# A third couple of groups in the up projections, later restores of the residual, parking at first chunks

## The chip, the cores and the metric

One core of a Trainium2 chip runs the whole program. The metric is device microseconds from the first to the last instruction of one launch, as the median of several runs; less is better.

## The reference

The program computes two layers of a streaming encoder on 256 positions of width 2048, batch 1, all in float32. Each layer is a token mixer and a gated feed-forward part, each followed by a residual and a layer norm:

```python
for i in range(DEPTH):                       # DEPTH = 2
    m = gmlp_mixer(x, ...) if i % 2 == 0 else mla_mixer(x, ...)
    x = layer_norm(ALPHA * x + m, ln_mix_g[i], ln_mix_b[i])
    f = conv_ffn(x, ffn_w_up[i], ffn_conv_w[i], ffn_conv_b[i], ffn_w_down[i])
    x = layer_norm(ALPHA * x + f, ln_ffn_g[i], ln_ffn_b[i])
```

The change concerns the feed-forward part, `conv_ffn`: `h = x @ w_up` (2048 x 11008), a causal depthwise convolution of width 3 over the positions of `h`, then `(silu(g) * a) @ w_down` with `a` and `g` the two halves of `h` (5504 each).

## The kernel before

**Products.** TensorE multiplies in a reduced float32 form, so each weight chunk `raw` (1 MB, read on SyncE's DMA queue, SP) is split in two parts: ScalarE casts it to `wh` (line 134) and VectorE subtracts, `wl = raw - wh` (line 137). The activations `xhl` are kept as such pairs too. `Feed.next` hands out the next chunk and lets the loads run up to four chunks and the splits two chunks ahead.

**Up projection.** Its columns come in 22 groups (0 to 21) of 4 chunks each (the last is half a group). Group 0 is done beside the layer norm ahead of it (`boundary`). The others are *plain* or in *couples*, as the table `UP` says. A plain group (`plain`) multiplies each chunk 16 times with 512 columns for `wh` and 256 for `wl`, accumulates four tiles `up{layer}_{group}_{f}`, and ends with two `pair`s: sum of halves `h_`, convolution `c_`, `silu`, and product into `act`. A couple (`summed`) takes 8 chunks of two groups. Four of them go as in `eight`, 24 matmuls of 512 columns. The other four (`UP_SEVEN`) use a scheme of seven products in place of eight, 21 matmuls of 512 columns; for them VectorE also makes sums of weight blocks, `ts` (line 144), and splits those into `th` and `tl`, and it needs combined inputs `xu`, made beforehand by `combine_up` (one `upy`, four `xsu`, one cast and one `xu`). After a couple come `rest` and four adds on VectorE, then, behind the first chunk of the next plain group, 16 transposes (`turn_back`, tiles `upr`), and the couple's four `pair`s behind its second and third chunk (`both`).

**Side work, by a table.** `EARLY` maps (group, chunk) to steps done beside the plain groups: `restore f` scales and shifts a quarter `f` of the residual that the layer norm left unscaled (its gain and bias rows `lnp` are DMA loads, then two multiplies and two adds of 128x512), `combine i` is above, and `park h` writes a half of the residual to DRAM on GpSimd's queue (`resd`), after which its room (tiles `res` and `sum`) is free. The other side work is `jobs`: eight chunks of the later down projection ("parked", `praw`, numbers 231 to 266) are loaded, split as for seven products (`pwh`, `pwl`, `pth`, `ptl`), and written to DRAM (`keptwh`, ...), one step at a time, 31 steps in all.

**Order.** Each engine works in the order of its own instruction stream, which follows from the order of these calls and from the scheduler of the framework. Rooms come from pools by tag: "big" has 14 of 2048 columns, "side" 6, "raw" 3. `behind(load)` asks that a load be queued after the latest matmul so far; it adds no wait.

Layer 0's up projection has chunks 144 to 229. Chunks 148 to 151 are group 1, and 152 to 155 group 2.

Of the kernel before, what the change touches and what calls it, by code (L numbers as in the profile page):

```python
# [15 lines left out]
P = 128  # L16
# [53 lines left out]
LEAD = 5  # L70
KEEP = {"wide": 4, "seven": 6, "parked": 6}

UP = [(1,), (2,), (3,), (4,), (5, 6), (7,), (8, 9), *((i,) for i in range(10, 22))]
UP_PAIRS = [0, 2, 1, 3, 5, 4, 6, 7]
UP_SEVEN = (2, 3, 4, 6)
EARLY = {(1, 2): ("restore", 0), (2, 1): ("combine", 0), (2, 2): ("restore", 1), (2, 3): ("park", 0),
         (3, 1): ("restore", 2), (3, 2): ("combine", 1), (3, 3): ("restore", 3), (4, 0): ("park", 1),
         (4, 1): ("combine", 2), (4, 2): ("combine", 3)}


def plan(n_k):
# [140 lines left out]
def trunk(ctx: ExitStack, tc: tile.TileContext, x, xT, gm_in, gm_wout, ffn_up, ffn_dn,  # L222
# [12 lines left out]
    def slot(shape, name, dt=F32, tag="big"):  # L235
        return big.tile(shape, dt, tag=tag, name=name, bufs=SLOTS[tag])
# [13 lines left out]
    def behind(ins):  # L250

        if recent[0] is not None and feed.used > 0:
            order(ins, recent[0])
# [424 lines left out]
    class Norm:  # L678
# [53 lines left out]
        def restore(self, f):  # L732

            row = []
            for j in range(2):
                t = tp.tile([P, 512], F32, tag="t2", name=f"lnp{self.idx}_{f}{j}", bufs=T2)
                src = ln_rows[2 * self.idx + j : 2 * self.idx + j + 1, f * 512 : (f + 1) * 512]
                (nc.gpsimd if self.idx == 1 else nc.sync).dma_start(t, src.to_broadcast([P, 512]))
                row.append(t)
            for b in range(2):  # L740
                nc.vector.tensor_tensor(self.r(b, f), self.r(b, f), row[0], ALU.mult)
                nc.vector.tensor_tensor(self.r(b, f), self.r(b, f), row[1], ALU.add)
# [287 lines left out]
    def ffn(layer, ln, acc, end, last):  # L1030
# [39 lines left out]
        def combine_up(p):  # L1070

            x = xhl[p // 2][:, p % 2 * 2 : p % 2 * 2 + 2]
            y = tp.tile([P, 2, S], F32, tag="t2", name=f"upy{layer}_{p}", bufs=T2)
            nc.vector.tensor_tensor(y, x[:, :, 0:S].bitcast(F32), x[:, :, S : 2 * S].bitcast(F32), ALU.add)
            if len(sums) % 2 == 0:
                rooms.append(slot([P, 2, 8 * P], f"xu{layer}_{p}", F32R))
            sums[p] = combine(f"u{layer}_{p}", rooms[-1][:, len(sums) % 2, :], y[:, 0], y[:, 1])

        early = {"restore": old.restore, "park": old.park, "combine": lambda i: combine_up(UP_SEVEN[i])}
# [1 line left out]
        def plain(gi, turned):  # L1081

            nt, nk = (4, 4) if gi < 21 else (2, 8)
            acc = [bank(f"up{layer}_{gi}_{f}") for f in range(nt)]
            for c in range(KD // nk):
                hi, lo = feed.next()
                prod_a(acc, xhl, range(nk * c, nk * c + nk), hi, lo)
                if c == 0 and turned:
                    for i, t in enumerate(turned[2]):
                        turn_back(turned[1][i % 2], t, i // 2)  # L1090
                if turned and 0 < c < 3:
                    both(turned[0][c - 1], turned[1][c - 1])
                if (gi > 9 and c > 0) or (gi, c) == (7, 3):
                    next(jobs, None)
                if (gi, c) in FIRST:
                    acts.make(*plan(NF_FF)[0][FIRST.index((gi, c))])
                if gi == 1 and c == 0:
                    after(1, 1, None)
                    both(0, hb)
                if (gi, c) in EARLY:  # L1100
                    name, i = EARLY[gi, c]
                    early[name](i)
            for f in range(nt // 2):
                pair(2 * gi + f, acc[f], acc[nt // 2 + f])
# [456 lines left out]
```

## Time and profile before

| what | value |
|---|---|
| median of 3 runs | 2450.4 us (2450.39 to 2450.6) |
| profiled execution, its own time | 2449.38 us |
| its span, first to last instruction | 2447.3 us |
| granted TensorE clock | 1.00 |
| busy: TensorE / VectorE / ScalarE / GpSimd | 100% / 90% / 62% / 6% |
| DMA over the span, mean | 256 GB/s |

Times in views of the profile count from the start of the span. Layer 0's up projection lies between about 780 and 1264 us, layer 1's from about 1735 on. PE is TensorE, DVE VectorE, ACT ScalarE, POOL GpSimd, SP SyncE. A duration of an instruction includes its way through the engine, so two that follow each other overlap a little. L137 is line 137 of the kernel before; in the changed kernel all lines from 739 on stand two lower down.

### The profile page before, as it was taken

The page shows a single profiled execution, that of the slowest core. Times are in us where ns is not written, and L with a number is a line of the kernel's source. Part 1 is how long each engine was busy: PE and PEld are TensorE (multiplying, and loading weights), DVE is VectorE, ACT ScalarE, POOL GpSimd, SP SyncE. Part 2 cuts the span into 40 slices and gives each one's busy share as a digit, 9 for nine tenths or more (in the row PEclk, how much of TensorE's full clock was granted, in tenths as well). Part 3 has the DMA queues.
Part 4 walks back from the last instruction along what each step waited for, and adds up shares of the span by engine and source line. Part 5 has one row for each costly group of instructions (what it writes and reads, how often), then busy time and mean ns, then how long its engine had stood idle before and what let it go on. Part 6 is the DMA issues. An engine that isn't in the chain of part 4 may idle for free.

```text
span 2447.3 us, 32249 instructions
## 1 busy us (share of the span) xinstructions
PE 2440.4 (100%) x12151; PEld 2065.3 (84%) x12151; DVE 2191.0 (90%) x2914; ACT 1512.4 (62%) x1997; POOL 140.6 (6%) x261
## 2 busy tenths in 40 slices
PE   9999999999999999999999999999999999999999
PEld 7888888888888888888888888988888888888887
DVE  7999999899998889998889897878798999888998
ACT  6666665566576655666665566665655666666553
POOL 0000000001010000011000000000000001010000
PEclk9999999999999999999999999999999999999999
DMA  7555666658796755799988885533575589898894
GB/s 293 203 205 205 233 202 205 207 173 304 254 296 241 239 205 194 258 359 374 341 318 320 320 298 172 188 141 126 207 272 184 181 323 375 321 371 300 314 353 178
DMA packets 128763, 627.37 MB, mean 256 GB/s; under 512 B 11592, under 2 KB 15184, under 8 KB 91616
## 3 DMA queue, kind: packets, MB, share of 16 engines
q1 hardware_dynamic: 94224, 462.47, 53.5%
q0 software_dynamic: 34384, 162.86, 17.9%
q8 instruction: 95, 1.56, 0.3%
q14 instruction: 60, 0.49, 0.1%
HBM read 552.35 MB, written 72.93 MB: 256 GB/s over the span
## 4 chain that ended last, share of the span: by engine, by line
PE 97%; DVE 1%; DMA 1%; ACT 0%; issue 0%; POOL 0%; ACTq 0%; DVEq 0%; POOLq 0%
PE up L242 30%; PE ub L242 16%; PE dn_q L242 8%; PE dn_p L242 6%; PE v_q L242 5%; PE v_p L242 4%; PE up_q L242 3%; PE up_p L242 3%; PE wo_q L242 2%; PE dn_e L242 2%; PE wo_p L242 2%; PE upf L242 2%; PE mo L242 2%; PE v_e L242 2%; PE mkv L242 1%; PE qn L242 1%
## 5 line engine op out<-in xcount | busy, mean ns | idle before, releaser
L137 DVE TENSOR_TENSOR wl<-raw,wh 128x1024 fp32r<-128x1024 f32 (+5 forms) x611 | 936.3, 1550 | 108.9 <-ACT wh L134 77.4
L134 ACT CAST wh<-raw 128x1024 fp32r<-128x1024 f32 (+5 forms) x611 | 790.9, 1318 | 307.2 <-PE up L242 67.8
L242 PE MATMUL up<-xhl,wh 128*128 128x512 f32 x2112 | 492.9, 390 | 0.0
L242 PEld LDWEIGHTS up<-xhl,wh 128*128 128x128 f32 x2112 | 392.3, 188 | 78.7
L134 ACT CAST th<-ts 128x1536 fp32r<-128x1536 f32 x196 | 203.7, 1051 | 173.9 <-DVE ts L144 144.2
L242 PEld LDWEIGHTS up<-xhl,wl 128*128 128x128 f32 x2112 | 262.4, 192 | 5.1
L242 PE MATMUL up<-xhl,wl 128*128 128x256 f32 x2112 | 265.1, 283 | 0.0
L137 DVE TENSOR_TENSOR tl<-ts,th 128x1536 fp32r<-128x1536 f32 x196 | 231.6, 1219 | 7.9 <-ACT th L134 3.3
L242 PE MATMUL ub<-wh,xhl 128*128 128x512 f32 x552 | 172.0, 393 | 0.0
L144 DVE TENSOR_TENSOR ts<-ts,raw 128x512 f32<-128x512 f32 x196 | 134.7, 687 | 2.0
L242 PEld LDWEIGHTS ub<-wh,xhl 128*128 128x128 f32 x552 | 103.6, 188 | 23.2 <-issue 1.9
L144 DVE TENSOR_TENSOR ts<-raw 128x1024 f32<-128x1024 f32 x98 | 119.5, 1219 | 2.2 <-DMA raw<-in_gm_in_dram 0.8
L242 PE MATMUL ub<-wl,xhl 128*128 128x512 f32 x276 | 107.5, 389 | 0.0
L242 PE MATMUL v_q<-wh,xhl 128*128 128x512 f32 x224 | 70.8, 391 | 0.0
L242 PEld LDWEIGHTS ub<-wl,xhl 128*128 128x128 f32 x276 | 51.8, 188 | 10.9
L242 PE MATMUL v_p<-wh,xhl 128*128 128x512 f32 x192 | 59.9, 389 | 0.0
L242 PEld LDWEIGHTS v_q<-wh,xhl 128*128 128x128 f32 x224 | 42.1, 188 | 9.7 <-ACT wh L134 0.9
L832 ACT ACTIVATE lny<-lnt,lncol 128x128 f32<-128x128 f32 x96 | 36.6, 471 | 15.7 <-PE lnt L828 15.6
L161 DVE TENSOR_TENSOR praw<-praw 128x512 f32<-128x512 f32 x64 | 43.9, 686 | 0.5
L242 PE MATMUL v_q<-wl,xhl 128*128 128x512 f32 x112 | 43.6, 389 | 0.0
L242 PE MATMUL mo<-wh,oT 128*128 128x512 f32 x128 | 42.7, 411 | 0.0
L242 PEld LDWEIGHTS v_p<-wh,xhl 128*128 128x128 f32 x192 | 36.0, 188 | 7.5
(2073 smaller groups left out, 4824.9 us busy)
## 6 DMA issues: line engine op xcount, KB each, us to landing
raw<-in_ffn_up_dram SPq DMA_DIRECT2D x172, 1024.0 KB, 5.9
raw<-in_gm_in_dram SPq DMA_DIRECT2D x93, 1024.0 KB, 5.3
raw<-in_ffn_dn_dram SPq DMA_DIRECT2D x68, 1024.0 KB, 7.7
raw<-in_gm_wout_dram SPq DMA_DIRECT2D x48, 1024.0 KB, 6.4
praw<-in_ffn_dn_dram POOLq DMA_DIRECT2D x16, 1024.0 KB, 12.5
keptth<-pth POOLq DMA_DIRECT2D x16, 1024.0 KB, 8.5
kepttl<-ptl POOLq DMA_DIRECT2D x16, 1024.0 KB, 8.7
fth<-keptth POOLq DMA_DIRECT2D x16, 1024.0 KB, 9.5
```

What stands on the lines that cost most here:

```text
L134: cast = self.nc.scalar.copy(hi, raw)
L137: self.nc.vector.tensor_tensor(lo, raw, hi.bitcast(F32), ALU.subtract)
L144: add = lambda o, a, b: self.nc.vector.tensor_tensor(o, a, b, ALU.add)
L161: add = lambda o, a, b: pin(nc.vector.tensor_tensor(o, a, b, ALU.add))
L242: recent[0] = nc.tensor.matmul(o, l, r, start=start, stop=stop, skip_group_check=True)
L832: nc.scalar.activation(y[:, j], t[:, j * P : (j + 1) * P], AF.Identity, bias=lncol[:, o : o + 1], scale=lncol[:, g : g + 1])
```

## The change

```diff
-UP = [(1,), (2,), (3,), (4,), (5, 6), (7,), (8, 9), *((i,) for i in range(10, 22))]
+UP = [(1,), (2,), (3, 4), (5,), (6, 7), (8,), (9, 10), *((i,) for i in range(11, 22))]
 UP_PAIRS = [0, 2, 1, 3, 5, 4, 6, 7]
 UP_SEVEN = (2, 3, 4, 6)
-EARLY = {(1, 2): ("restore", 0), (2, 1): ("combine", 0), (2, 2): ("restore", 1), (2, 3): ("park", 0),
-         (3, 1): ("restore", 2), (3, 2): ("combine", 1), (3, 3): ("restore", 3), (4, 0): ("park", 1),
-         (4, 1): ("combine", 2), (4, 2): ("combine", 3)}
+EARLY = {(1, 1): ("restore", 0), (1, 2): ("combine", 0), (1, 3): ("combine", 1), (2, 0): ("restore", 1),
+         (2, 1): ("combine", 2), (2, 2): ("park", 0), (2, 3): ("combine", 3),
+         (12, 0): ("restore", 2), (14, 0): ("restore", 3), (14, 2): ("park", 1)}
@@ Norm.restore
-                (nc.gpsimd if self.idx == 1 else nc.sync).dma_start(t, src.to_broadcast([P, 512]))
+                load = (nc.gpsimd if self.idx == 1 else nc.sync).dma_start(t, src.to_broadcast([P, 512]))
+                if f > 1 and self.idx != 1:
+                    behind(load)
@@ ffn, combine_up
-                rooms.append(slot([P, 2, 8 * P], f"xu{layer}_{p}", F32R))
+                rooms.append(slot([P, 2, 8 * P], f"xu{layer}_{p}", F32R, "side"))
@@ ffn, plain
-                if (gi > 9 and c > 0) or (gi, c) == (7, 3):
+                if (gi > 10 and (c > 0 or 15 < gi < 19)) or (gi, c) == (8, 3):
                     next(jobs, None)
```

In both layers the couples become (3,4), (6,7) and (9,10) where they were (5,6) and (8,9). The four combines, restores 0 and 1 and the first park move into groups 1 and 2; restores 2 and 3 and the second park move to groups 12 and 14. Parking starts with one step in group 8 and goes on from group 11 (before: 7 and 10), and in groups 16 to 18 it also has a step at the first chunk; it ends at the same place. The rooms of `xu` come from "side" instead of "big".

The first place is VectorE after the convolutions of group 1. Before, chunks 157 to 159 are plain ones of groups 3 and 4 and stand among the restores of the residual:

```order
L742 TENSOR_TENSOR res0_0_4680<-res0_0_4680,lnp0_11_6545 128x512
L137 TENSOR_TENSOR wl157_6552<-raw157_6459,wh157_6551 128x1024 x2
L741 TENSOR_TENSOR sum0_1_5777<-sum0_1_5777,lnp0_20_6715 128x512 x2
L742 TENSOR_TENSOR sum0_1_5777<-sum0_1_5777,lnp0_21_6717 128x512
L137 TENSOR_TENSOR wl158_6636<-raw158_6509,wh158_6635 128x1024 x2
L742 TENSOR_TENSOR sum0_1_5777<-sum0_1_5777,lnp0_21_6717 128x512
L1074 TENSOR_TENSOR upy0_3_6763<-xhl1_1_5899 128x512
L137 TENSOR_TENSOR wl159_6676<-raw159_6557,wh159_6675 128x1024
```

With the change, behind the same convolutions (an upy and its xsu are a combine, ts and tl belong to a seven-product chunk):

```order
L1076 TENSOR_TENSOR upy0_4_6520<-xhl1_2_5900 128x512
L137 TENSOR_TENSOR wl156_6531<-raw156_6438,wh156_6530 128x2048
L314 TENSOR_TENSOR xsu0_4_6523<-upy0_4_6520 128x128
L315 TENSOR_TENSOR xsu0_4_6523<-upy0_4_6520 128x128
L144 TENSOR_TENSOR ts157_6570<-raw157_6486 128x1024
L316 TENSOR_TENSOR xsu0_4_6523<-xsu0_4_6523,upy0_4_6520 128x128
L144 TENSOR_TENSOR ts157_6570<-ts157_6570,raw157_6486 128x512
L317 TENSOR_TENSOR xsu0_4_6523<-upy0_4_6520,xsu0_4_6523 128x128
L137 TENSOR_TENSOR wl157_6572<-raw157_6486,wh157_6571 128x1536
L326 TENSOR_TENSOR xu0_4_6522<-xsu0_4_6523,xu0_4_6522 128x512
L137 TENSOR_TENSOR tl157_6574<-ts157_6570,th157_6573 128x1536
L137 TENSOR_TENSOR tl157_6574<-ts157_6570,th157_6573 128x512
```

The last two combines now stand between the splits of the first couple, the second half of the residual is not touched here any more, and chunk 157 has become a seven-product chunk.

The second place is group 12. On SyncE's queue the rows of restore 2 stand behind the load of chunk 196:

```order
L109 DMA raw195_8273<-in_ffn_up_dram 128x2048
L109 DMA raw196_8363<-in_ffn_up_dram 128x2048
L738 DMA lnp0_20_8397<-in_ln_rows_dram 128x512
L738 DMA lnp0_21_8399<-in_ln_rows_dram 128x512
L109 DMA raw197_8411<-in_ffn_up_dram 128x2048
```

Before, they stood there behind the load of chunk 157, ahead of that of 158. On VectorE the restore itself now stands between the parking of chunk 231 (praw, ptl), the convolutions of group 11 and the split of chunk 195:

```order
L161 TENSOR_TENSOR praw231_7740<-praw231_7740 128x512
L1028 SCALAR_TENSOR_TENSOR c_0a22_8319<-h_0a22_8317,cst_176,c_0a22_8319 128x254
L411 TENSOR_TENSOR h_0g22_8325<-up0_11_2_8071,lo_0g22_8323 128x256
L743 TENSOR_TENSOR sum0_1_5777<-sum0_1_5777,lnp0_20_8397 128x512 x2
L744 TENSOR_TENSOR sum0_1_5777<-sum0_1_5777,lnp0_21_8399 128x512
L173 TENSOR_TENSOR ptl231_8308<-praw231_7740,pth231_8307 128x2048
L1026 SCALAR_TENSOR_TENSOR c_0g22_8327<-h_0g22_8325,cst_176,c_0g22_8327 128x255
L744 TENSOR_TENSOR sum0_1_5777<-sum0_1_5777,lnp0_21_8399 128x512
L1028 SCALAR_TENSOR_TENSOR c_0g22_8327<-h_0g22_8325,cst_176,c_0g22_8327 128x254
L137 TENSOR_TENSOR wl195_8406<-raw195_8273,wh195_8405 128x1024
```

Here a multiply and an add of the residual came into a place that had none.

## Prediction, made before the changed kernel ran

> **What bounds the kernel now.** I read the page first: busy shares, then the chain of waits.
>
> ```profile
> span 2447.3 us, 32249 instructions
> PE 2440.4 (100%) x12151; PEld 2065.3 (84%) x12151; DVE 2191.0 (90%) x2914; ACT 1512.4 (62%) x1997; POOL 140.6 (6%) x261
> PE 97%; DVE 1%; DMA 1%; ACT 0%; issue 0%; POOL 0%; ACTq 0%; DVEq 0%; POOLq 0%
> ```
>
> TensorE (PE) is busy almost throughout and is 97% of the chain. So matmuls taken away come back as time, but VectorE (DVE), which prepares every operand and stands at 90%, has little to lend. Which of the two decides is seen in the stage, so next I read the chain through layer 0's up projection (start, duration, what) and the same rows of layer 1.
>
> ```profile
> 816.36 83.36 PE up L242 x480
> 899.72 1.36 PE up_q L242 x6
> ...
> 939.16 1.36 PE up_q L242 x6
> 940.52 5.54 PE up L242 x32
> 946.06 1.75 PE upr L1049 x16
> 947.81 16.68 PE up L242 x96
> 964.49 1.36 PE up_q L242 x6
> ...
> 1005.64 5.54 PE up L242 x32
> ```
> ```profile
> 1771.00 83.36 PE up L242 x480
> 1900.70 1.75 PE upr L1049 x16
> ```
>
> The chain never leaves PE here: 480 plain matmuls without a gap, then couple (5,6) from 899.72 to 940.52, 16 transposes, a plain group, couple (8,9) from 964.49 to 1005.64. Layer 1 repeats the 83.36 and the 1.75, so I cost one layer and double it. Third, the busy time by stretch: groups 2, 3, 4, couple (5,6), groups 11 and 12, and groups 11 to 20 together (columns: PE, PEld, DVE, ACT, POOL busy, granted clock, DMA share, GB/s).
>
> ```profile
> 833.60:855.80 22.20, 22.20 (x130) 19.66 (x129) 21.15 (x36) 12.48 (x20) 0.55 (x1) 1.00 0.89 296
> 855.80:878.00 22.20, 22.20 (x129) 19.67 (x128) 20.80 (x41) 12.58 (x20) 1.26 (x2) 1.00 0.70 240
> 878.00:899.70 21.70, 21.70 (x127) 19.26 (x126) 17.63 (x26) 10.67 (x17) 0.00 (x0) 1.00 0.67 223
> 899.70:940.50 40.80, 40.80 (x182) 33.78 (x181) 37.04 (x43) 25.36 (x27) 0.00 (x0) 1.00 0.53 185
> 1029.60:1051.80 22.20, 22.20 (x130) 19.66 (x129) 20.29 (x29) 13.17 (x17) 2.87 (x5) 1.00 0.98 362
> 1051.80:1074.10 22.30, 22.30 (x130) 19.75 (x129) 20.67 (x29) 13.75 (x20) 2.88 (x5) 1.00 1.01 420
> 1118.50:1140.80 22.30, 22.30 (x130) 19.73 (x129) 19.30 (x28) 13.37 (x20) 1.78 (x3) 1.00 0.99 383
> 1029.60:1251.90 222.30, 222.30 (x1282) 196.90 (x1281) 195.86 (x274) 142.09 (x196) 22.61 (x40) 1.00 0.94 357
> ```
>
> PE fills every stretch at clock 1.00. DVE's cover is 1 to 4 us per group, and DMA is nearly full from group 11 on. These two are what the change draws on.
>
> **What goes: matmuls.** A group is 4 chunks of 32 matmuls, so by the 480-matmul row it takes 83.36 x 128/480 = 22.23 us, two of them 44.46. A couple takes 940.52 - 899.72 = 40.80 and its transposes 1.75. One more couple per layer gains 44.46 - 42.55 = 1.91 us, both layers **3.82 us**. That is the most the change can give: nothing else on PE becomes less. The Trainium skill's "TensorE: Matmul & The Clock Gate", section "Back-to-back issue gap", gives an isolated matmul of N columns N/2.4 + 2.5 ns, which would make the gain about 1.0 us an estimate per layer (128 pairs of 512 and 256 columns against 180 of 512). The 1.36 us for six are 227 ns each, not 216, so the measured rows decide.
>
> **What moves forward: DVE before the first couple.** Couple (3,4) starts 44.46 us earlier than (5,6) did, at 899.72 - 44.46 = 855.26, and four combines must be done by then. The orders of DVE agree up to the subtraction at 822.94. I count from there to the last difference (`tl`) of chunk 162, the fourth seven-product chunk. Three wide chunks of 24 x 0.227 = 5.44 and three seven-product ones of 21 x 0.227 = 4.76 precede it on PE, and PE wants that second part some 2.5 us into the chunk: 855.26 + 30.6 + 2.5 = 888.4, which leaves 65.5 us.
>
> ```profile
> 808.58 3.49 DVE L137 TENSOR_TENSOR wl<-raw,wh 128x1024 fp32r<-128x1024 f32 x3
> 822.94 1.22 DVE L137 TENSOR_TENSOR wl<-raw,wh 128x1024 fp32r<-128x1024 f32 x1
> 824.41 1.29 DVE L741 TENSOR_TENSOR res<-res,lnp 128x512 f32<-128x512 f32 x2
> 832.80 0.42 DVE L411 TENSOR_TENSOR h_0a<-up,lo_0a 128x256 f32<-128x256 f32 x1 [0.76 <-ACT lo_0a L409]
> 839.58 0.48 DVE L1024 SCALAR_TENSOR_TENSOR c_0a<-h_0a,cst,c_0a 128x255 f32<-128x255 f32 x1 [0.47 <-ACT c_0a L1023]
> 846.54 0.42 DVE L1041 TENSOR_TENSOR act<-s,c_0a 128x256 f32<-128x256 f32 x1 [0.28 <-ACT s L1040]
> 847.82 2.36 DVE L137 TENSOR_TENSOR wl<-raw,wh 128x1024 fp32r<-128x1024 f32 x2 [0.25 <-PE up L242]
> 872.01 2.36 DVE L137 TENSOR_TENSOR wl<-raw,wh 128x1024 fp32r<-128x1024 f32 x2 [0.17 <-issue]
> 875.70 0.28 DVE L317 TENSOR_TENSOR xsu<-upy,xsu 128x128 f32<-128x128 f32 x1
> 875.90 0.28 DVE L315 TENSOR_TENSOR xsu<-upy 128x128 f32<-128x128 f32 x1
> 880.69 1.23 DVE L137 TENSOR_TENSOR wl<-raw,wh 128x1024 fp32r<-128x1024 f32 x1 [3.85 <-DMA resd<-sum]
> 886.59 2.29 DVE L137 TENSOR_TENSOR wl<-raw,wh 128x2048 fp32r<-128x2048 f32 x1
> 894.50 0.43 DVE L1041 TENSOR_TENSOR act<-s,c_0a 128x256 f32<-128x256 f32 x1
> 894.85 1.75 DVE L137 TENSOR_TENSOR wl<-raw,wh 128x1536 fp32r<-128x1536 f32 x1
> 896.52 2.35 DVE L137 TENSOR_TENSOR tl<-ts,th 128x1536 fp32r<-128x1536 f32 x2
> ```
>
> Instructions overlap, so I count start to start: 1.135 us per 1024 columns (three in 3.49, the last 1.22), 0.60 per 512 (1.29 for two), 1.67 per 1536 (894.85 to 896.52), 2.2 per 2048 (886.59 to the next at 888.80), 0.20 per 128, 0.35 per `act`, and for the convolutions' two-step pairs 0.39, their durations of 0.48 less the same overlap. Before chunk 162's end the new order has 7 half splits (7.9 us), 3 whole ones (6.6), four seven-product chunks (1.14 + 2 x 0.60 + 1.67 + 1.67 + 0.60 = 6.28 each, 25.1), four combines (2 x 0.60 + 4 x 0.20, some 2.2 with their small gaps; 8.8), 8 restore operations (4.8), and 8 `h`, 16 convolution and 5 `act` operations (10.7). Together 64.0 of the 65.5 us. If DVE idles as long as now without the wait for the residual's store (0.76 + 0.47 + 0.28 + 0.25 + 0.17 = 1.93 us), PE stalls 64.0 + 1.93 - 65.5 = 0.4. If it idles with the 3.85 too, 4.3. With no idling, nothing. I take **0.4**, since the store of the other half, now issued earlier in group 2, held up no DVE instruction in any of these rows; the bounds are 0 and 4.3.
>
> **Third couple.** Couple (8,9) took 1005.64 - 964.49 = 41.15, 0.35 over (5,6): only one plain group lies ahead of it, and the four convolutions and adds of the couple before fall there. Couples (6,7) and (9,10) now both lie so. One more such stall: **0.35**, bounds 0 and 0.70.
>
> **Late residual rows, groups 11 to 13.** Restore 2 goes to group 12's first chunk, where a couple's pairs and the first parking steps already stand on DVE. Its four operations take 2.4 us, and group 11 of before had 22.20 - 20.29 = 1.9 us free. If nothing else gave, the stall would be 0.5; DVE runs up to two chunks ahead, so some is absorbed. The rows that it needs are now loaded behind chunk 196.
>
> ```profile
> DMA to landing us min/median/max: 4.9/6.2/7.3
> raw<-in_ffn_up_dram SPq DMA_DIRECT2D x37, 1024.0 KB, 8.8
> keptth<-pth POOLq DMA_DIRECT2D x8, 1024.0 KB, 8.6
> praw<-in_ffn_dn_dram POOLq DMA_DIRECT2D x6, 1024.0 KB, 12.8
> ```
>
> The first row is the loads of these rows in groups 1 to 3, the others are issues from group 11 to the end of the stage. The load can go out once chunk 193's split has freed a room, and on DVE 9.9 us of work then lie ahead of the restore (`act` and four convolution steps 1.9, chunk 194 2.3, half of 195 1.1, and the rest up to it). At 6.2 to 8.8 us plus issue the rows come just in time; at 12.8 DVE waits 2.9 us, with the splits of 195 to 198 queued behind it and PE behind those. I take **0.4** for both, bounds 0 and 2.9. Restore 3 and the second park, at group 14, have one couple's pairs fewer beside them. The park's store frees the room for chunk 205's split: 8.6 us by the `keptth` row against the 11 us that two chunks last, as the 3.85 us at 880.69 cost PE nothing, so 0.
>
> **Denser parking, groups 16 to 18.** Thirty-one steps, starting one group later and ending at the same place, put four into each of three groups. With a step in every chunk and four steps per parked chunk, a group asks for 4 raw loads, one `praw` and stores of 2 x 1024 and 2 x 768 KB: 8704 KB, 8.91 MB in 22.23 us or 401 GB/s, against the mean of 357. Group 12 moved 420 in 22.30 us. I take **0.1**; bounds 0 and 3.0, the latter if three such groups get only the 383 GB/s of the 1118.50 row, whose DMA share was already 0.99: 26.74 MB/383 = 69.8 us against 66.7. The fourth step is a quarter of a parked chunk's DVE work (1.67 + 4 x 0.60 + 2.2 = 6.3), 1.6 us, and the 1118.50 row leaves 3.0 free.
>
> **Rest, at nothing.** The rooms of the combined inputs change from one pool to another that is empty of parked chunks until group 8; were it short, only the first `praw` would be late. The first half's rows land as before.
>
> **Sum.** Per layer -1.91 + 0.4 + 0.35 + 0.4 + 0.1 = -0.66 us, both -1.3. The profiled execution took 2449.38 us, its span 2447.3 plus 2.1 around it; by it 2448.1. The median of the runs is 2450.4 (2450.39 to 2450.6), 1.0 above it, so the forecast is 2450.4 - 1.3 = **2449.1 us**.
>
> **Rivals.** *Full gain*: DVE's run-ahead swallows all four terms, 2450.4 - 3.8 = 2446.6. For it: PE is at 22.20 of 22.20 in the stretches with DVE at 21.15. Against it: couple (8,9) did lose 0.35. 20%.
>
> *DMA full in groups 16 to 18*: the 3.0 instead of 0.1, per layer +2.2, 2454.9. For it: shares of 0.99 to 1.01 at 383 and 420 GB/s. Against it: the 420. 7%. With the long mean of 357 as the true limit, the three groups last 26.74/0.357 = 74.9 us, 8.2 over, and the time is 2450.4 + 2 x 7.4 = 2465; group 12 speaks against it, 1%. The Trainium skill's "DMA: Bandwidth & Descriptors", section "Where 436 GB/s comes from", states such a limit, about 358 GB/s for transfers between HBM and SBUF; the 420 in group 12 disagrees with it as a limit of this core.
>
> *Slower, the first couple waits for DVE*: the 4.3 of above instead of 0.4, per layer +3.2, both +6.5, 2456.9. Its place is chunk 162, its mechanism the store of the first residual half that now frees a room for chunk 157's casts just as the couple's operands are made; ScalarE waits for it with the third combine's cast queued behind. From 2.6 us of idle time on DVE between 822.94 and 888.4 the kernel is slower than before (a stall of 1.1 uses up what the other terms leave of the 1.91), from 5.0 us by over 0.2%. For it: the 3.85 wait of the same kind. Against it: a store of that size took 8.6 us in busier groups, and by the same spacings some 11 us of DVE work lie between the restore and the first operand that needs chunk 157's cast. 10%.
>
> **How the numbers follow.** Forecast 62%, full gain 20%, DMA 8%, slower 10%. The forecast's own range, its four terms between 0 and twice their size, is 2446.6 to 2451.6. The range to hold 8 in 10 goes from 2446.4 to 2453.2: the full gain with 0.2 for the runs' spread, and above it partial sizes of the two slow cases; their far ends, about 15%, are left out. A measurement of this kernel tells about 0.2%, 4.9 us, from no change, so 2445.5 to 2455.3 is the same. The full gain lies within it: faster 3%. Slower needs the last rival or the 357 limit, 8%. Same 89%.
>
> **What would show it.** After: PE rows of couples at 855, 920 and 985 us; `up` matmuls before the first falling from 480 to about 224; the first couple 40.8 to 41.2 long, with a stall at chunk 162 if any; groups 12 and 13 over 22.23; groups 16 to 18 near 400 GB/s with PE still full. A couple over 42 us, or a `wl` or `th` waiting for the residual's store by more than 3 us, would make the prediction wrong; so would a gain over 3.8.

## The result, and the profile after

The changed kernel takes **2467.74 us** (median of 6 runs, 2465.74 to 2469.43) beside 2450.5 for the kernel before: **ratio 1.0070, interval 1.0058 to 1.0083**. It is 17 us slower, where 2449.1 was forecast in a range of 2446.4 to 2453.2. The profiled execution took 2465.74 us with a span of 2463.7. First its page:

```profile
span 2463.7 us, 32050 instructions
PE 2442.6 (99%) x12031; PEld 2061.3 (84%) x12031; DVE 2221.7 (90%) x2938; ACT 1518.3 (62%) x1983; POOL 140.2 (6%) x261
PE 80%; DVE 10%; DMA 5%; ACT 2%; issue 2%; SPq 0%; ACTq 0%; DVEq 0%
```

PE was 97% of the chain and is 80%: VectorE, DMA and ScalarE have come into it. The 120 matmuls are gone (12151 to 12031), yet PE's busy time has grown by 2 us, a first sign that some matmuls run slower. Where, the chain through layer 0's up projection shows (start, duration, what):

```profile
816.73 38.90 PE up L242 x224
855.63 1.36 PE up_q L242 x6
...
896.58 5.54 PE up L242 x32
902.12 1.75 PE upr L1051 x16
...
920.54 1.36 PE up_q L242 x6
...
961.67 5.54 PE up L242 x32
...
985.63 1.36 PE up_q L242 x6
...
1026.43 5.54 PE up L242 x32
...
1042.99 1.11 issue
1044.10 1.75 DVE pwl L173
1048.60 7.94 DMA raw<-in_ffn_up_dram
...
1271.89 1.36 PE dn_q L242 x6
```

The three couples are nearly perfect: 40.95, 41.13 and 40.80 us, and at their end (1026.43) the layer is 209.70 us past its 816.73. Before, the end of group 10 came 83.36 + 40.80 + 23.97 + 41.15 + 23.97 = 213.25 us past its 816.36 (a group with transposes is 5.54 + 1.75 + 16.68 = 23.97). That is 3.55 more; the third couple's transposes, 1.75, are still to come, so **1.80 us are gained by then**. From there on the chain leaves PE, and the first down product comes at 1271.89, 455.16 us past 816.73; before, 1012.93 + 250.06 - 816.36 = 446.63. So 8.53 us are lost in sum, **10.3 us of them behind the third couple**. In layer 1:

```profile
1779.74 38.91 PE up L242 x224
...
1989.43 5.54 PE up L242 x32
...
2234.06 1.36 PE dn_q L242 x6
```

The same: 1989.43 - 1779.74 = 209.69, then 2234.06 - 1779.74 = 454.32 against 2217.67 - 1771.00 = 446.67 before, so 7.65 lost in sum, 9.5 behind the couples. The two layers together, 16.2, are nearly all of the span's growth of 16.4. Next PE itself, in order of time (start, duration, matmuls, and in brackets the idle time ahead and its releaser):

```profile
1109.43 3.03 PE L242 MATMUL up<-xhl,wl 128*128 128x256 f32 x24
1115.71 1.21 PE L242 MATMUL up<-xhl,wl 128*128 128x256 f32 x8 [3.24 <-DVE wl L137]
1116.76 9.04 PE L242 MATMUL up<-xhl,wh 128*128 128x512 f32 x32
...
1217.98 1.22 PE L242 MATMUL up<-xhl,wl 128*128 128x256 f32 x8 [0.39 <-DVE wl L137]
...
1252.98 1.80 PE L242 MATMUL up<-xhl,wl 128*128 128x256 f32 x8 [2.35 <-DVE wl L137]
1255.23 1.88 PE L242 MATMUL up<-xhl,wl 128*128 128x256 f32 x8 [0.45 <-DVE wl L137]
```

PE waits for VectorE mainly in two places: at the last chunk of group 14 and, near the end of the stage, at the last chunk of group 20 (with a short wait in group 19). The waits are 3.24 + 0.39 + 2.35 + 0.45 = 6.4 of the 10.3 us. Of the other 3.9, some 2.8 are slow matmuls: behind the first wait 32 of them take 9.04 us, elsewhere 7.44, and the two groups of eight at the end take 1.80 and 1.88, elsewhere 1.22 beside a wait. The rest is the broken stream itself, about 0.26 at each of the four waits: 32 such matmuls take 3.84 us from start to start without a break (1042.75 to 1046.59), eight of them 0.96. What VectorE did ahead of that first wait:

```profile
1105.41 0.47 DVE L1028 SCALAR_TENSOR_TENSOR c_0g<-h_0g,cst,c_0g 128x254 f32<-128x254 f32 x1
1108.96 1.29 DVE L743 TENSOR_TENSOR sum<-sum,lnp 128x512 f32<-128x512 f32 x2 [3.08 <-DMA lnp<-in_ln_rows_dram]
...
1112.11 1.29 DVE L744 TENSOR_TENSOR sum<-sum,lnp 128x512 f32<-128x512 f32 x2 [1.18 <-DMA lnp<-in_ln_rows_dram]
...
1114.44 1.22 DVE L137 TENSOR_TENSOR wl<-raw,wh 128x1024 fp32r<-128x1024 f32 x1
```

It stands still for the rows of restore 3 (two multiplies and two adds, as restore 2 has in group 12), and the split that PE needs (`wl` at 1114.44) is queued behind. For the rows of restore 2 it had waited only 0.42 us. The four loads of layer 0 took longer than in groups 1 to 3 (minimum, median, maximum):

```profile
DMA to landing us min/median/max: 8.9/10.1/13.0
```

### The profile page after: what moved, and what is told of

It is laid out like the page before. It is cut to its first block, busy times and chain, and to the rows that moved or that the text cites. A ratio compares the mean times of both kernels' runs of the same rounds, so it can differ in the third digit from the quotient of the medians.

```text
span 2463.7 us, 32050 instructions
## 1 busy us (share of the span) xinstructions
PE 2442.6 (99%) x12031; PEld 2061.3 (84%) x12031; DVE 2221.7 (90%) x2938; ACT 1518.3 (62%) x1983; POOL 140.2 (6%) x261
## 4 chain that ended last, share of the span: by engine, by line
PE 80%; DVE 10%; DMA 5%; ACT 2%; issue 2%; SPq 0%; ACTq 0%; DVEq 0%
PE ub L242 16%; PE up L242 10%; PE dn_q L242 8%; PE dn_p L242 6%; PE v_q L242 5%; PE up_q L242 5%; DVE wl L137 4%; PE up_p L242 4%; PE v_p L242 4%; DMA raw<-in_ffn_up_dram 3%; PE wo_q L242 2%; PE dn_e L242 2%; PE wo_p L242 2%; PE upf L242 2%; PE mo L242 2%
## 5 line engine op out<-in xcount | busy, mean ns | idle before, releaser
L137 DVE TENSOR_TENSOR wl<-raw,wh 128x1024 fp32r<-128x1024 f32 (+4 forms) x595 | 929.7, 1578 | 96.0 <-ACT wh L134 79.7
L134 ACT CAST wh<-raw 128x1024 fp32r<-128x1024 f32 (+4 forms) x595 | 785.8, 1342 | 279.3 <-DMA raw<-in_ffn_up_dram 81.8
L242 PE MATMUL up<-xhl,wh 128*128 128x512 f32 x1856 | 436.6, 392 | 1.0 <-ACT wh L134 1.0
L242 PEld LDWEIGHTS up<-xhl,wh 128*128 128x128 f32 x1856 | 346.6, 189 | 71.2 <-ACT wh L134 1.4
L134 ACT CAST th<-ts 128x1536 fp32r<-128x1536 f32 x212 | 220.7, 1052 | 201.5 <-DVE ts L144 176.7
L137 DVE TENSOR_TENSOR tl<-ts,th 128x1536 fp32r<-128x1536 f32 x212 | 250.5, 1217 | 4.2 <-PE v_p L242 1.9
L242 PE MATMUL up<-xhl,wl 128*128 128x256 f32 x1856 | 237.4, 285 | 12.3 <-DVE wl L137 12.3
L242 PEld LDWEIGHTS up<-xhl,wl 128*128 128x128 f32 x1856 | 232.9, 193 | 18.4 <-DVE wl L137 13.8
L242 PE MATMUL up_q<-wh,xhl 128*128 128x512 f32 x192 | 59.5, 389 | 0.0
L242 PE MATMUL up_p<-wh,xhl 128*128 128x512 f32 x192 | 59.1, 389 | 0.0
L242 PEld LDWEIGHTS v_q<-wh,xhl 128*128 128x128 f32 x224 | 42.0, 188 | 10.3 <-ACT wh L134 1.7
```

What stands on the lines that cost most here:

```text
L134: cast = self.nc.scalar.copy(hi, raw)
L137: self.nc.vector.tensor_tensor(lo, raw, hi.bitcast(F32), ALU.subtract)
L242: recent[0] = nc.tensor.matmul(o, l, r, start=start, stop=stop, skip_group_check=True)
```

## The experiments

Every kernel was timed beside the kernel before on the same chip. The column "against before" is the difference of the medians.

| kernel | median us | against before | ratio, 95% interval |
|---|---|---|---|
| changed kernel | 2467.74 | +17.2 | 1.0070 (1.0058 to 1.0083) |
| late restores only, on before | 2456.37 | +6.5 | 1.0026 (1.0016 to 1.0036) |
| parking only, on before | 2454.35 | +4.5 | 1.0018 (1.0009 to 1.0028) |
| changed, no first-chunk steps | 2471.15 | +21.3 | 1.0091 (1.0076 to 1.0106) |
| changed, rows not behind products | 2454.79 | +5.0 | 1.0021 (1.0011 to 1.0030) |
| changed, no late restores | 2448.11 | -2.5 | 0.9988 (0.9979 to 0.9997) |
| changed, restores in groups 5 and 8 | 2451.75 | +1.2 | 1.0006 (0.9997 to 1.0016) |
| changed, no parked sums | 2452.37 | +1.8 | 1.0007 (0.9997 to 1.0017) |
| changed, half the stores | 2450.80 | +0.2 | 1.0002 (0.9992 to 1.0011) |
| restores on GpSimd, groups 5 and 8 | 2456.70 | +6.6 | 1.0029 (1.0019 to 1.0038) |
| restores on GpSimd, groups 12 and 14 | 2464.55 | +14.4 | 1.0053 (1.0038 to 1.0069) |
| restores at last chunks of 5 and 8 | 2451.77 | +1.6 | 1.0006 (0.9997 to 1.0015) |
| changed, rows' loads earlier | 2466.79 | +16.6 | 1.0064 (1.0050 to 1.0078) |
| restores in 5, 5 and 8 by halves | 2450.88 | +0.7 | 1.0002 (0.9993 to 1.0011) |
| restores at second chunks of 5 and 8 | 2452.05 | +1.9 | 1.0005 (0.9997 to 1.0014) |
| restores at first chunks of 5 and 8 | 2451.73 | +1.6 | 1.0004 (0.9996 to 1.0013) |
| restore work without rows | 2456.05 | +5.9 | 1.0024 (1.0014 to 1.0033) |
| rows and waits without work | 2455.34 | +5.2 | 1.0024 (1.0014 to 1.0033) |

**Which part of the change.** Two kernels put one part on the kernel before, two take one part from the changed kernel.

Late restores only, on the kernel before (with the `behind` of the change):

```diff
-         (3, 1): ("restore", 2), (3, 2): ("combine", 1), (3, 3): ("restore", 3), (4, 0): ("park", 1),
-         (4, 1): ("combine", 2), (4, 2): ("combine", 3)}
+         (3, 2): ("combine", 1), (4, 1): ("combine", 2), (4, 2): ("combine", 3),
+         (12, 0): ("restore", 2), (14, 0): ("restore", 3), (14, 2): ("park", 1)}
```

> The kernel before (couples and parking as before) with only restores 2 and 3 and the second park moved to groups 12 and 14, their rows queued behind products. Theory R (the rows' loads, issued into a full DMA, land 9 to 15 us later and hold up VectorE, which costs PE 3.2 to 3.7 us at group 14 and some 2 us of clock behind it): that stall shows here too, some 4 to 6 us per layer, 2458 to 2462 us. Theory D (the denser parking of groups 16 to 18 is what makes DMA and VectorE late): no stall, 2449 to 2452 us.

Parking only, on the kernel before:

```diff
-                if (gi > 9 and c > 0) or (gi, c) == (7, 3):
+                if (gi > 10 and (c > 0 or 15 < gi < 19)) or (gi, c) == (8, 3):
```

> The kernel before with only the parking moved (one step in group 8, then from group 11, with first chunks in groups 16 to 18). Theory R: at most a small stall, 2450 to 2452 us. Theory D: the stall of 2 to 3 us near groups 20 and 21 and its loss of clock show here, 4 us or more per layer, 2457 to 2462 us.

The changed kernel without the steps at first chunks:

```diff
-                if (gi > 10 and (c > 0 or 15 < gi < 19)) or (gi, c) == (8, 3):
+                if (gi > 10 and c > 0) or (gi, c) == (8, 3):
```

> The changed kernel without the parking steps at first chunks of groups 16 to 18, so that parking ends one group later. Theory R: the stall at group 14 stays as it is, the one at groups 20 and 21 goes or shrinks: per layer -1.9 + 3.4 + 2 for the clock, about 2457 to 2461 us. Theory D: both go, 2447 to 2451 us.

The changed kernel without the order of the rows:

```diff
-                if f > 1 and self.idx != 1:
-                    behind(load)
```

> The changed kernel without the order of the late rows behind products; the scheduler then queues the four loads of a layer around chunk 192, one group ahead of the first restore and two and a half ahead of the second. Theory R: VectorE no longer waits for them, the stall at group 14 goes, 2447 to 2453 us depending on whether the one at group 21 was a consequence. Theory D: both stalls stay, 2462 to 2468 us.

The late restores alone cost 6.5 us even without a third couple, a little under theory R's figures; but the stall that theory R names is not there in layer 0. VectorE waits 3.2 us for rows, and PE's one wait in the stage, 1.45 us, comes in group 16. Freeing the rows gives back 12 of the 17 us and ends 1.8 us over theory R's range; its trace has no wait for rows in either layer, and the stall at group 14 is gone, while waits of 1.80 us in group 12 and 2.9 us in group 20 are left in layer 0. The two runs on parking were worse tests than meant. On the kernel before, group 8 belongs to a couple, so the one step planned there is never made and the last of the 31 falls into group 20. The changed kernel without first-chunk steps likewise goes on parking to the end of group 20. In both, VectorE is then late where the down projection begins (waits of PE: total, times, longest), in the first, where four such waits make 2.7 us,

```profile
PE dn_p L242 <- DVE h_1g L411: 1.0, 1, 1.0
```

and in the second, where four make 8.4,

```profile
PE dn_p L242 <- DVE h_0a L411: 4.6, 2, 3.0
```

So they tell what parking costs if it ends later, and not what the denser steps cost. That comes out of the next run.

**Is it the restores?** The changed kernel without restores 2 and 3 (rows and arithmetic; the second half of the residual is not restored):

```diff
-         (12, 0): ("restore", 2), (14, 0): ("restore", 3), (14, 2): ("park", 1)}
+         (14, 2): ("park", 1)}
```

> The changed kernel with restores 2 and 3 left out altogether, rows and arithmetic (the scaling and shifting of the residual's second half is not computed), the second park kept at group 14. Theory R (rows' latency is the main cause): no stall at group 14, and at most the one at groups 20 and 21 left, like the kernel without the order behind products or better, 2448 to 2453 us. Theory V (VectorE has no reserve left in groups 11 to 20, whatever delays it): the same runs, but the 4.8 us of restore work gone also clears the end of the stage, 2446 to 2449 us. Theory D (DMA): the stage is as late as before, 2455 us or more.

This is faster than before, by 2.5 us of the 3.8 that the matmuls are worth (the interval runs from 0.7 to 5.1 us; in its trace the first down products come 1.69 and 1.55 us earlier than before, counted from the start of the chain's plain `up` matmuls in each layer). Its chain (layer 0, from the third couple's transposes to the down projection; layer 1 has the same 227.83 us) and a stretch that is mostly group 18 (PE, PEld, DVE, ACT, POOL busy, clock, DMA share, GB/s):

```profile
1032.53 1.75 PE upr L1051 x16
1034.28 227.83 PE up L242 x1312
```
```profile
1181.40:1203.60 22.20, 22.20 (x129) 19.67 (x128) 19.10 (x27) 14.72 (x19) 2.86 (x5) 1.00 1.01 404
```

PE runs 1312 matmuls without a gap, through the groups with four parking steps, at 404 GB/s here and 391 and 329 in the two stretches before. So the third couple's gain is real, the denser parking by itself costs nothing, and **all of the loss hangs on restores 2 and 3**: 2467.7 against 2448.1. But it doesn't come from them alone. At the same places they cost 6.5 us on the kernel before and 19.6 here, so about 13 us come from their meeting a stage that the third couple and the parking have filled. The rival of a DMA limit of 357 GB/s, which gave 2465, came near the measured time for a wrong reason.

**Work or wait?** Loading the rows earlier was to separate the two.

```diff
-         (12, 0): ("restore", 2), (14, 0): ("restore", 3), (14, 2): ("park", 1)}
+         (11, 1): ("fetch_rows", 2), (12, 0): ("restore", 2), (13, 0): ("fetch_rows", 3), (14, 0): ("restore", 3),
+         (14, 2): ("park", 1)}
```

> The changed kernel, with only the loads of the late rows moved forward by three and four chunks (to group 11's second chunk and group 13's first), still behind products; the restores stay in groups 12 and 14. If the rows' late landing is most of the cost: VectorE doesn't wait for rows, the stall at group 14 goes, 2452 to 2456 us. If the rows' lateness is only a sign of VectorE being behind: 2462 to 2468 us.

It didn't separate them: the scheduler moved part of the restores' operations forward with their rows (half of restore 3 by some 25 us), and VectorE waited for them about as long as before (4.7 us in the changed kernel, here

```profile
DVE sum L750 <- DMA lnp<-in_ln_rows_dram: 4.4, 1, 4.4
```

in layer 0). So two kernels hold the places nearly fixed. In the one, the eight operations of a layer stand in the same chunks but work on numbers in place, each quarter on its neighbour (so the residual is not the reference's); in the other, the rows are loaded and waited for, and each operation touches 4 columns (so the half is not restored).

```diff
+            late = f > 1 and self.idx != 1
...
-            for j in range(2):
+            for j in range(0 if late else 2):
...
-                nc.vector.tensor_tensor(self.r(b, f), self.r(b, f), row[0], ALU.mult)
-                nc.vector.tensor_tensor(self.r(b, f), self.r(b, f), row[1], ALU.add)
+                x = self.r(b, 5 - f) if late else None
+                for row_, op in ((0, ALU.mult), (1, ALU.add)):
+                    step = nc.vector.tensor_tensor(self.r(b, f), self.r(b, f), x if late else row[row_], op)
+                    if late:
+                        behind(step)
```

> The changed kernel with restores 2 and 3 working on other numbers that are in place (each quarter multiplied by and added to its neighbour, so the residual is not the reference's): the same eight operations at the same places of VectorE's order, no rows, no loads, no waits for them. If VectorE has no reserve left, 4.8 us of work a layer comes back as about as much at PE: 2448 + 7 to 10, 2455 to 2458 us. If only the waits cost: 2448 to 2450 us.

```diff
+            n = 4 if f > 1 and self.idx != 1 else 512
...
-                nc.vector.tensor_tensor(self.r(b, f), self.r(b, f), row[0], ALU.mult)
...
+                nc.vector.tensor_tensor(self.r(b, f)[:, 0:n], self.r(b, f)[:, 0:n], row[0][:, 0:n], ALU.mult)
...
```

> The changed kernel with the late rows loaded and waited for as before, but each late restore operation on 4 columns in place of 512 (so the second half of the residual is not restored): the waits without the work. If a wait costs as work does, 4.5 to 5 us a layer, the time is 2455 to 2459 us and the stall at group 14 stays, perhaps smaller. If the work is what costs: 2448 to 2450 us.

Both cost. Against the kernel without restores, the work alone is worth 5.9 + 2.5 = 8.4 us, the waits alone 5.2 + 2.5 = 7.7. Together they would make 2.5 less than their sum, +13.6; the changed kernel has +17.2, but each of these differences is known only to 2 or 3 us, so the 3.6 between them is not clear of the noise. Per layer the work is 4.8 us of VectorE by the prediction's own spacing and costs 4.2; the waits are 3.2 us on VectorE in the second kernel's layer 0 and 4.0 in layer 1, and cost 3.9. The kernel with freed rows agrees: it does all the work, waits for no row, and lies 7.4 us over the kernel without restores, though its restore 3 stands some 30 us earlier. **On the mean, what VectorE loses here, PE loses, about one for one.** The busy times over 210 us of the stage (PE, PEld, DVE, ACT, POOL) say more. Before:

```profile
1030.00:1240.00 210.00, 210.00 (x1213) 186.06 (x1212) 187.01 (x261) 135.07 (x187) 22.61 (x40) 1.00 0.93 354
```

Changed, without restores:

```profile
1030.00:1240.00 210.00, 210.00 (x1221) 186.35 (x1220) 191.77 (x271) 138.35 (x190) 24.31 (x43) 1.00 0.94 360
```

Changed, with the work alone:

```profile
1030.00:1240.00 210.00, 209.63 (x1217) 185.72 (x1216) 190.33 (x267) 135.59 (x185) 22.24 (x39) 1.00 0.92 355
```

The changed kernel itself:

```profile
1030.00:1240.00 210.00, 206.37 (x1191) 182.63 (x1190) 187.31 (x263) 131.81 (x181) 21.70 (x38) 0.99 0.92 354
```

Without the restores, VectorE already works 4.8 us more than before in the same time; the largest parts are the third couple's four adds (2.7 us) and one more parking step (1.75). Given the restores' work too, its busy time doesn't rise, it falls a little: it does less of the other work instead, and PE comes less far (1221 matmuls, then 1217 and 1191). The 18 us in which VectorE is idle without the restores are, by the list of its waits, waits for ScalarE's casts and activations, and the extra work did not go into them.

Why idle time is no reserve here can be followed one step further. From 1029 to 1264 us ScalarE waited 12.7 us for raw chunks before, but 30.3 without the restores and 29.7 in the changed kernel. The load of a raw chunk waits for one of three rooms, which VectorE's splits set free (in the changed kernel SyncE's queue waits 194.8 us for them in these 235 us), and then takes some 9 us. So split, load, cast and split again form a loop, and what VectorE loses comes back to it as a later load. In the changed kernel's chain from 1026 to 1285 us these loads are the largest entry, 17.5%, ahead of VectorE's splits (15.8%) and PE's `up` matmuls (12.1%). No run changes the number of raw rooms, so the loop is read from the traces and not tested.

**Relief from either side.** Leaving out the four sums of each parked chunk (they are then not computed) takes 2.4 us of work a chunk from VectorE; not storing the parked chunks' low parts (the high ones are read in their place, so the down projection's products are not the reference's) takes 14 MB of writing a layer.

```diff
-                add(r[1], r[1], r[0])
-                add(r[0], r[0], r[2])
-                add(r[2], r[2], r[1])
-                add(r[3], r[3], r[2])
```

> The changed kernel with the four additions of each parked chunk left out (its sums of weight blocks are not computed; 2.4 us of VectorE a chunk, 19 us a layer), all transfers kept. Theory V: the stalls of both places go or nearly so, 2447 to 2452 us. Theory D: VectorE's work is not what is short, 2460 to 2468 us. Theory R: the group 14 stall stays, 2456 to 2462 us.

```diff
-            store(f"{n}l", lo, cols)
+            kept[f"{n}l"] = kept[f"{n}h"]
```

> The changed kernel with the low parts of the parked chunks not stored (the down projection then reads the high parts in their place, so its products are not the reference's): 14 MB less to write in each layer, VectorE's work unchanged. Theory D: rows and raw loads land earlier, stalls go, 2447 to 2453 us. Theory V: 2460 to 2468 us. Theory R: the rows' latency falls towards 7 us and the stall at group 14 with it, the one at the end stays, 2452 to 2460 us.

Both bring the time back to within 2 us of before. In the first VectorE waits longer for rows than in the changed kernel (6.6 us in layer 0 against 4.7), and yet in layer 0 only the local wait at group 14 is left,

```profile
1114.65 1.22 PE L238 MATMUL up<-xhl,wl 128*128 128x256 f32 x8 [1.77 <-DVE wl L137]
```

and the one in group 20 is gone, in layer 1 too: that one is the debt of the whole stage, paid at its end. Theory V's range is missed by 0.4 us. In the second, theory D's range held and theory V's, 2460 to 2468, failed. Its VectorE works more in the same 210 us than in any of the rows above, restores and all:

```profile
1030.00:1240.00 210.00, 209.44 (x1218) 185.72 (x1217) 193.00 (x272) 137.06 (x187) 15.36 (x26) 1.00 0.81 298
```

So 191.8 was not a limit of VectorE itself; how far its idle time can be used hangs on the traffic as well. The rows land sooner (median of layer 0's four, in the middle),

```profile
DMA to landing us min/median/max: 6.5/8.2/12.2
```

and VectorE waits 2.5 us for them in layer 0. But in layer 1 it waits 5.1 us for them, hardly less than the changed kernel's 5.5, while PE waits 0.8 us there in place of 6.8. What did change in both layers is the raw chunks: they land in 7.8 and 6.8 us (median) in place of 8.9 and 8.7, and ScalarE waits 26.0 and 13.6 us for them in place of 29.7 and 23.8. So in layer 1 the relief does not come by the rows; that it comes by the raw loads fits these numbers but was not tested alone.

**Other places for the restores.** The first two of these were restores 2 and 3 at the last chunk of group 5 and in group 8, then at the last chunks of both with a late park:

```diff
+         (5, 3): ("restore", 2), (8, 0): ("restore", 3), (8, 3): ("park", 1)}
```

> The changed kernel with restore 2 at group 5's last chunk, restore 3 and the second park in group 8 (the rows still ordered behind products), where DMA moves 190 to 195 GB/s. Theory R: the rows land in 5 to 7 us, no stall at group 14, 2448 to 2453 us. Theory V: 2448 to 2452 us too if groups 5 and 8 have the reserve; if they have not, the couples behind them stall, 2453 to 2460 us.

```diff
+         (5, 3): ("restore", 2), (8, 3): ("restore", 3), (11, 3): ("park", 1)}
```

> The changed kernel with restore 2 at group 5's last chunk and restore 3 at group 8's last, the second park at group 11's last. Theory V: the couples (6,7) and (9,10) behind them lose part of VectorE's run-ahead, some 0.5 to 1 us per restore: 2449 to 2452 us; more than that only if the later park holds a room that groups 9 to 11 need, 2453 us or more.

Then three more, by halves, at second chunks, and at first chunks:

```diff
+         (5, 1): ("restore", 2), (5, 2): ("first", 3), (8, 1): ("second", 3), (8, 3): ("park", 1)}
```

> The changed kernel with restore 2 at group 5's second chunk, restore 3 by halves at group 5's third and group 8's second chunk, the second park at group 8's last. Theory V says that the place counts: VectorE idles most behind the couples. If these chunks have idle time left after the couple's pairs, 2448 to 2450 us; if the work comes too late to use it, as at the groups' last chunks, 2451 to 2453 us.

```diff
+         (5, 1): ("restore", 2), (8, 1): ("restore", 3), (8, 3): ("park", 1)}
```

> As the one before, with both restores whole, at the second chunks of groups 5 and 8: 2448 to 2450 us by the same reason if group 8 has as much room as group 5, else 2450 to 2453 us.

```diff
+         (5, 0): ("restore", 2), (8, 0): ("restore", 3), (8, 3): ("park", 1)}
```

> Both restores at the first chunks of groups 5 and 8, ahead of the couple's pairs, where VectorE stood idle 3 us for rooms. Their rows can be loaded only when the couple's tiles are free, behind its transposes, so VectorE may wait some 2 us for them. 2447.5 to 2450 us if this idle time covers both wait and work; 2452 us or more if the wait for the rows is added to the pairs behind it.

All five lie between +0.7 and +1.9 us, not to be told from before and 15 to 16.5 us better than the change. Theory V's better cases, 2450 us or less, were not reached: the restores there cost 3.2 to 4.4 us over the kernel that leaves them out, 1.6 to 2.2 a layer for 4.8 us of work, so the groups between the couples have little reserve as well. The 3 us of idle time that the last expectation counts on are not there in the changed kernel: VectorE waits 2.2 us in group 5, and in group 8 it is busy 23.7 of 23.9 us (DMA moves 195 and 228 GB/s in the two).

Last, the restores on GpSimd:

```diff
-                nc.vector.tensor_tensor(self.r(b, f), self.r(b, f), row[0], ALU.mult)
...
+                eng = nc.gpsimd if f > 1 and self.idx != 1 else nc.vector
+                eng.tensor_tensor(self.r(b, f), self.r(b, f), row[0], ALU.mult)
...
```

The first of the two kernels also has restore 2 at (5, 0), restore 3 at (8, 0) and the second park at (8, 2).

> The changed kernel with restores 2 and 3 computed on GpSimd instead of VectorE, started in groups 5 and 8, the second park in group 8. Theory V (what costs is restore work and waits in VectorE's queue, 4.8 us a layer that it has not): like the kernel without these restores, 2447 to 2449 us. Theory L (rows and rooms, not VectorE's work): like the restores in groups 5 and 8 on VectorE, about 2451 to 2452 us. Should GpSimd slow VectorE where both run, 2452 us or more.

> The changed kernel as it is, only restores 2 and 3 computed on GpSimd, rows still behind products. Then neither the rows' late landing nor the work stands in VectorE's queue. Theory V: 2447 to 2450 us. Should the rows' loads themselves be what harms (their place among the raw loads on SyncE's queue), the time stays above 2458 us. GpSimd also issues the parked chunks' loads and stores; should those become late behind the waiting restore, 2452 us or more.

Both lose, and theory V's ranges are missed. The trace shows that in groups 12 to 14 the work is not taken off VectorE in effect (its execution, 2470.08 us, was the slowest of four). GpSimd's own operations for restore 2 (start, duration of two)

```profile
1060.52 6.68 POOL L744 TENSOR_TENSOR sum<-sum,lnp 128x512 f32<-128x512 f32 x2 [10.68 <-DMA lnp<-in_ln_rows_dram]
1067.17 3.70 POOL L745 TENSOR_TENSOR sum<-sum,lnp 128x512 f32<-128x512 f32 x2
```

and VectorE's beside them:

```profile
1062.96 3.09 DVE L173 TENSOR_TENSOR ptl<-praw,pth 128x2048 fp32r<-128x2048 f32 x1 [0.21 <-ACT pth L172]
1065.98 1.51 DVE L1027 SCALAR_TENSOR_TENSOR c_0g<-h_0g,cst,c_0g 128x255 f32<-128x255 f32 x1
1067.41 2.31 DVE L137 TENSOR_TENSOR wl<-raw,wh 128x1024 fp32r<-128x1024 f32 x1
```

Each of the three is about 1 us longer than elsewhere (2.29, 0.48 and 1.22), 2.9 together, where the four operations taken away are 2.4; and the stores of the parked chunk were queued on GpSimd behind 10.7 us of waiting. In groups 5 and 8 the larger loss was of another kind: the second park, put in the middle of group 8, made VectorE wait

```profile
984.94 1.76 DVE L137 TENSOR_TENSOR wl<-raw,wh 128x1536 fp32r<-128x1536 f32 x1 [4.87 <-DMA resd<-sum]
```

for the room, right in couple (9,10), which cost PE 3.75 us in layer 0. So that run doesn't test its theory.

## Why the prediction was wrong

**The step that failed** is "Late residual rows, groups 11 to 13": "I take 0.4 for both, bounds 0 and 2.9", and with it "Restore 3 and the second park ... so 0". Measured in the place of 0.4 per layer: 10.3 and 9.5 us. Three things in it were wrong.

It asked of one group at a time whether VectorE had room ("group 11 of before had 1.9 us free", "some is absorbed"). But the free time of these stretches is waiting, and what is late in one group isn't made up in the next; the debt of groups 12 to 19 comes due in group 20. Over the stage, VectorE had worked 187 of 210 us before; the third couple and the parking add 4.8, and the restores ask for 4.8 again. The first 4.8 cost PE nothing, the second about as much as they are. Where between them the reserve ends, the trace before could not say.

It gave restore 3 nothing, though its rows are loaded in the same way as those of restore 2. For restore 2 "just in time" was right: VectorE waited 0.42 us for its rows in layer 0 and 0.51 in layer 1. For restore 3 it waited 4.3 and 5.0 us, more than the bound of 2.9 that was set for restore 2. The loads, four of each layer, landed in 8.7 to 15.2 us.

And it had no price for what a wait of PE costs beyond its length, 3.9 us in layer 0 and 2.7 in layer 1: a slower clock for a while (last section) and the broken stream.

**The other steps held.** The gain of 1.91 per layer shows as 1.80 at the end of the third couple, and the couples begin at 855.63, 920.54 and 985.63, as forecast (855, 920, 985). The first couple's 0.4 was 0.15; the rival that put its slow side there, at 4.3 us, did not come: chunk 162 brought no wait of note, and nothing waited for the first half's store. The third couple lost nothing, the second 0.33. The denser parking's 0.1 was 0 by the kernel without restores, and the DMA rivals fell with it. Without its 0.4 for the late rows the forecast's own sum gives 2450.4 - 2.1 = 2448.3, and that kernel took 2448.1; that it comes so close is partly luck, since the terms of the first couple and the parking were smaller than taken. (In the DMA rival, 69.8 us against 66.7 is 3.1 and not 3.0, which changes nothing.) The signs that the prediction named looked past the place: groups 12 and 13 kept their 22.23 us, groups 16 to 18 ran full at 359 to 385 GB/s, and the stalls came in groups 14 and 20. So the slower side of the range was covered by mechanisms that did not act, and left open for the one that did.

## What to carry to other kernels

Before work is moved into a stage, sum the busy time of the helper engine over the whole stage and ask whether it has ever been higher there. If not, a reserve is neither shown nor excluded: here 4.8 us more were free and the next 4.8 were not. Its idle time counts as reserve only if a run shows that time shrinking under more work, and the loads it waits for, at one remove, belong to the count. A load that an in-order engine waits for has to be priced by its landing time in the traffic of its new place, once for every load, and with all that is queued behind it. And work on a path that is 97% one engine is best tested by leaving it out: one run without the restores would have told gain and loss apart at once.

## What the hardware showed unexpectedly

**A short wait can cost PE more than its length.** The granted clock ahead of the 3.24 us wait, right behind it, and after that (seventh figure: the clock), in the changed kernel:

```profile
1105.00:1112.00 7.00, 7.00 (x43) 6.22 (x42) 2.85 (x6) 3.44 (x6) 0.00 (x0) 1.00 1.02 393
1115.70:1120.00 4.30, 4.29 (x16) 3.61 (x17) 4.30 (x8) 2.30 (x3) 0.00 (x0) 0.63 1.02 354
1120.00:1125.00 5.00, 5.00 (x23) 4.06 (x23) 5.00 (x5) 3.62 (x3) 0.53 (x1) 0.98 0.55 193
```

In the kernel with the work alone, the last waits of layer 0 are 2.67 and 0.18 us, and the clock behind them

```profile
1248.50:1253.00 4.50, 3.93 (x16) 3.64 (x17) 4.50 (x9) 3.42 (x5) 0.00 (x0) 0.50 1.06 423
1253.00:1258.00 5.00, 5.00 (x20) 4.04 (x19) 2.29 (x4) 1.58 (x2) 0.00 (x0) 0.79 1.06 411
```

is half of full speed for 4.5 us and more. Its layer 0 lost some 6.8 us against the kernel without restores, with waits of 3.1. Read in finer windows, the clock in the changed kernel is at half for 3.4 us behind each of three waits (3.24 and 2.35 us in layer 0, 3.65 in layer 1), and in this kernel for 6.8 us; half clock for 3.4 us is worth 1.7 us of matmuls. The Trainium skill's "TensorE: Matmul & The Clock Gate", section "What's actually happening", describes this: half clock after an idle window of about 3.4 us, full clock after a busy one. The 0.50 agrees; that waits of 2.67 us or less were enough here does not fit a window that has to be wholly idle. Nor does the length of a wait decide it alone: one of 2.58 us in layer 1 of the kernel without parked sums left the clock at 1.00, while two of 1.03 and 1.04 us, close together, brought it to 0.66 over the next 5 us in the kernel with restores at the last chunks. What decides isn't shown.

**GpSimd beside VectorE.** The restore's operations on GpSimd, 687 ns each on VectorE, took 1.3 to 3.3 us, and lengthened the operations of VectorE that ran beside them by about 1 us each. The Trainium skill's "GPSIMD Engine Reference", section "Specifications", says that the two share the interfaces to SBUF and contend when VectorE has two inputs there, as the rows above show.
